# One 512-column matmul for two 256-column ones in the first block of a two-block transformer kernel

## The chip, the cores and the metric

The kernel runs on one core of one Trainium2 chip. The metric is device time in microseconds (us) of that core, from the first to the last instruction with what lies around them. Times are medians of several executions; the profile is of one further execution. PE is the matmul engine (TensorE), PEld its weight loads, DVE is VectorE, ACT is ScalarE, POOL is GpSimd, SP issues most transfers.

## What is computed

256 tokens of 2048 features go through two blocks. Only the first is touched by the change:

```python
z = rmsnorm(h, g) @ w_in                       # 2048 x 8704: conv, q, k, v and gate columns
y_a = (b_a * centred_dwconv3(c_a * v_a, w)) @ w_out_a      # 1024 x 2048
y_b = banded_window_attention(rope(q), rope(k), v, sink) @ w_o_attn   # 1024 x 2048
h = h + (sigmoid(gl_a + b) * y_a + sigmoid(gl_b + b) * y_b) @ w_mix_out
up = centred_dwconv3(rmsnorm(h, g2) @ ffn_w_up, w) + b     # 2048 x 11264
h = h + (silu(up[:, :5632]) * up[:, 5632:]) @ ffn_w_down   # 5632 x 2048
```

The second block has a convolution, attention and a layer of 16384 experts, of which each token takes 128.

## The kernel before

Everything is fp32. For the matmul each operand is cut into a high part (type fp32r, a copy by ScalarE) and a low part (the rest, a subtraction by VectorE), and a product is the sum of three: high by high, high by low and low by high. An activation chunk of 128 features lies in SBUF as 512 columns: 256 tokens of high parts, then 256 tokens of low parts. `split` (L263) and `prep` (L343) write it so.

Weights come as tiles of 512 KB (`wtile`, L400): 512 input by 256 output features. `wsplit` (L388) starts the transfer from SP (four buffers), copies the high part on ACT (L396) and subtracts on DVE (L397), into three buffers each. `gemm` (L411) takes one weight tile: for both halves `j` of 128 output features and four chunks `k` of 128 input features it calls `three` (L403), which issues three matmuls of 256 columns into the same 256 columns of PSUM, each with a weight load of its own: high weights by high activations (L405), high weights by low activations (L408), low weights by high activations (L409). These 24 matmuls use up one weight tile. `proj` (L420) makes 256 output features: four weight tiles (two for w_oa and w_ob), one PSUM bank of 512 columns (two halves of 256 tokens).

PSUM holds the pool `pmm` with four tiles of one bank, `psc` (two banks, attention scores) and `ptp` (two banks). A result leaves PSUM by one instruction in most places: `scaled` (L379) multiplies 512 columns by a factor per token on DVE; `add_residual` (L620) adds 512 columns to the residual `hT` on DVE; q and k are copied by ACT in halves (L557); the convolution's inputs and the outputs of w_oa and w_ob (L584, L585, L615, L616) are read by DVE where they are used.

The order of the first block is: k, q and v projections with rotation (L531 to L566); eight convolution projections, each with one unit of attention behind it (L581); four projections w_b (L589); eight rounds of w_ga, w_gb, w_oa, w_ob (L603); eight w_mix projections that update `hT` and prepare the next input (L627); the feed-forward part in six groups of 8, 8, 8, 8, 8 and 4 up-projections (L687). A group's down-projection (`down`, L663: eight outputs, each of two weight tiles, and of one in the last group) is issued after the first up-projection of the next group. Behind each of the last group's eight outputs stands `finish` (L676), which prepares the second block's input and two sums of squares. A scheduler fixes each engine's order when the program is built; on the chip each engine then works its queue in order.

The second block and the experts use the same `gemm` and the same pool (`proj`, `proj32`, `out_half` at L802, and the loop over the first expert table at L1039). The loop over the second expert table (L1220) has matmuls of 512, 512 and 448 columns into six banks.

Of the kernel before, what the change touches and what calls it, by code (L numbers as in the profile page):

```python
# [77 lines left out]
def arrange(inp):  # L78
    """Layout alone: the arrays that the program reads, by name."""
# [90 lines left out]
def constants():  # L170
    """Numbers that depend on shapes alone."""
# [34 lines left out]
def body(ctx: ExitStack, tc: tile.TileContext, a, out):  # L206
# [5 lines left out]
    pmm = pp.enter_context(tc.tile_pool(name="pmm", bufs=4, space=PSUM))  # L212
# [44 lines left out]
    def after(inst, other, wait=True):  # L257
        """inst waits for other, or only follows it on the same engine"""
# [13 lines left out]
    def rstd_of(v, pool, preload=True, out=None, lean=False):  # L272
        """v ** -0.5 with one Newton step; v [128, n] in SBUF; lean: less of it on the vector engine"""
# [26 lines left out]
    class MeanSquare:  # L300
        """mean of squares over the features, on all partitions: [128, T] in PSUM"""
# [4 lines left out]
        def feed(self, src, i, n=4, g=None):  # L306
            """chunks i * n to i * n + n of src, times g"""
# [35 lines left out]
    def prep(u, c, g):  # L343
        """chunk c of hT * g, split"""
# [4 lines left out]
    class Chunks:  # L349
        """[128, 16, 512] in two tiles"""  # L350
# [16 lines left out]
    def by_token(t, name):  # L367
        """[128, T], alike on all partitions -> [128 tokens, 2]"""
# [33 lines left out]

    def three(o, wh, wl, xh, xl, start, stop, behind=None):  # L403
        """o += w.T @ x without the product of the low parts"""
# [6 lines left out]
    def gemm(w, x, c0, ps, n_f, first, last, behind=None):  # L411
        """ps[:, j, :] += w[:, k, j].T @ x for 4 chunks of x from c0"""
# [7 lines left out]
    def proj(name, i, x, kt=4, c0=0):  # L420
        """256 features of a product, feature-major: [128, 2 * T] in PSUM"""
        ps = pmm.tile([P, 512], F32, tag="mm", name="ps_" + name)
# [4 lines left out]
    def proj32(name, i, x, g):  # L427
        """256 features of a product of x * g, x and the weights whole"""
        ps = pmm.tile([P, 512], F32, tag="mm", name="ps_" + name)
# [13 lines left out]
    def gemm_tok(w, x, c0, ps, col, f0, n, first, last):  # L443
        """ps[:, col + tt * n:][:n] += x[tt].T @ w[:, k, f0:f0 + n]: token-major"""
# [14 lines left out]
    def rope(src, dst, rotm, cos, sin):  # L459
        """dst = src * cos + rot(src) * sin, src in SBUF"""  # L460
# [65 lines left out]
    u = actin("u1")  # L526
    pk = pmm.tile([P, 512], F32, tag="mm", name="ps_k")
    for k in range(4):
        for c in range(4 * k, 4 * k + 4) if k < PREK else range(4 * k, DC) if k == PREK else ():
            prep(u, c, g_mix)  # L530
        gemm(wtile("w_kqv", k), u, 4 * k, pk, 2, k == 0, k == 3)  # L531
# [21 lines left out]
    for i in range(5):  # L553
        ps = proj("w_kqv", i, u) if i else pk
# [7 lines left out]
    ps = pmm.tile([P, 512], F32, tag="mm", name="ps_v")  # L562
    for k in range(4):
        gemm_tok(wtile("w_kqv", 20 + k), u, 4 * k, ps, 0, 0, 256, k == 0, k == 3)
    for tt in range(2):
        S.activation(vtok[:, tt], ps[:, tt * 256:(tt + 1) * 256], AF.Copy, scale=r1t[:, tt:tt + 1])  # L566

# [13 lines left out]
    for i in range(8):  # L581
        ps = proj("w_cv", i, u)
# [6 lines left out]
    for i in range(4):  # L589
        ps = scaled(proj("w_b", i, u), r1, "b_a")  # L590
# [12 lines left out]
    for i in range(8):  # L603
        pga = scaled(proj("w_ga", i, u), r1, "ga")
        pgb = scaled(proj("w_gb", i, u), r1, "gb")
        pya = proj("w_oa", i, ab, kt=2)
        pyb = proj("w_ob", i, ab, kt=2, c0=8)
        for j in range(2):
            c = 2 * i + j
            s = slice(j * T, (j + 1) * T)  # L610
            ga = tmp("g_a", "ta")
            S.activation(ga, pga[:, s], AF.Sigmoid, bias=bgate[:, c:c + 1])
            gb = tmp("g_b", "tb")
            S.activation(gb, pgb[:, s], AF.Sigmoid, bias=bgate[:, 16 + c:17 + c])
            V.tensor_tensor(ga, ga, pya[:, s], OP.mult)  # L615
            V.tensor_tensor(gb, gb, pyb[:, s], OP.mult)  # L616
            V.tensor_tensor(ga, ga, gb, OP.add)
            split(mix, c, ga)
# [44 lines left out]
    def down(gi, f, n, then=None):  # L663
        for i in range(8):
            ps = pmm.tile([P, 512], F32, tag="mm", name="ps_dn")
# [10 lines left out]
    def finish(i):  # L676
        """the input of the second block, of hT * g_fin"""
# [590 lines left out]
```

## Time and profile before

| | |
|---|---|
| runs (us) | 3041.73, 3041.75, 3043.57; median 3041.75 |
| span of the profiled execution | 3041.1 us |
| matmuls, weight loads | 22192, 22192 |
| PE, DVE, ACT, POOL busy | 98%, 76%, 50%, 28% of the span |
| mean granted TensorE clock | 0.996 |
| read from and written to HBM | 677.41 MB, 5.64 MB |

Busy time counts an engine from an instruction's start to its end. Matmuls are pipelined, so the duration of one (about 280 ns at 256 columns) is longer than the time from its start to the start of the next. What a stream of matmuls costs is read from the starts. A line of a helper stands for all of its calls, so groups are told apart by the tile that they write. Where a row says `x4`, it merges four instructions that follow each other.

### The profile page before, as it was taken

The numbers are of one execution on the slowest core, as the hardware profiler recorded it, in microseconds if no ns is written. First come the engines' busy times: TensorE is split into PE (matmuls) and PEld (weight loads), VectorE is DVE, ScalarE is ACT, GpSimd is POOL, SyncE is SP. The second block draws the span as 40 slices with busy tenths as digits, with TensorE's granted clock in tenths as the row PEclk, the third lists the DMA queues.
The fourth block names the chain that finished last, engine by engine and source line by source line (L and its number), as shares of the span: only waits on it lengthen the run. The fifth ranks groups of instructions, "written<-read, shape, count | busy, mean of one in ns | idle before, by whom it ended". The sixth has DMA issues, their size and how long they took to land.

```text
span 3041.1 us, 57181 instructions
## 1 busy us (share of the span) xinstructions
PE 2984.2 (98%) x22192; PEld 2825.3 (93%) x22192; DVE 2310.3 (76%) x4243; ACT 1529.6 (50%) x2229; POOL 866.0 (28%) x670
## 2 busy tenths in 40 slices
PE   8999999999999999999999999999999999999999
PEld 8889999999999999999988989999999897888887
DVE  6456555666666665668998788999997888999998
ACT  5454444554444444546555644555555554444444
POOL 0000000000000000000000055555554796777786
PEclk9999999999999999999999999999999999999999
DMA  6435555555555555554433678999999338999999
GB/s 220 147 121 182 184 181 186 182 180 182 185 183 183 185 181 185 182 182 165 154 110 126 212 248 298 318 321 325 324 319 330 124 135 299 337 332 339 330 335 319
DMA packets 211169, 686.81 MB, mean 226 GB/s; under 512 B 29264, under 2 KB 47056, under 8 KB 210512
## 3 DMA queue, kind: packets, MB, share of 16 engines
q1 hardware_dynamic: 169776, 523.15, 50.4%
q0 software_dynamic: 41120, 160.01, 15.3%
q8 instruction: 173, 2.83, 0.4%
q14 instruction: 100, 0.82, 0.1%
HBM read 677.41 MB, written 5.64 MB: 225 GB/s over the span
## 4 chain that ended last, share of the span: by engine, by line
PE 82%; DVE 6%; DMA 5%; issue 3%; POOL 2%; ACT 1%; POOLq 0%; SPq 0%; DVEq 0%; ACTq 0%
PE ps_w_up L408 6%; PE ps_w_up L409 6%; PE ps_w_up L405 6%; PE y L1240 5%; PE y L1239 5%; PE y L1238 5%; PE ps_u L409 3%; PE ps_u L405 3%; PE ps_dn L409 3%; PE ps_dn L405 3%; PE ps_dn L408 3%; PE ps_u L408 3%; DMA urows<-in_u_rows,ex 2%; PE ps_a L1160 2%; PE ps_sel L1121 1%
## 5 line engine op out<-in xcount | busy, mean ns | idle before, releaser
L397 DVE TENSOR_TENSOR wl<-wr,wh 128x1024 fp32r<-128x1024 f32 x572 | 700.6, 1225 | 403.0 <-ACT wh L396 397.5
L396 ACT ACTIVATE wh<-wr 128x1024 fp32r<-128x1024 f32 x572 | 606.3, 1060 | 739.3 <-PE ps_w_up L408 171.4
L907 POOL TENSOR_TENSOR tk_c<-tk_v 128x256 f32<-128x256 f32 x16 | 11.8, 740 | 1751.1 <-DVE tk_v L899 1750.9
L956 POOL DMA_INDIRECT vrows<-in_v_rows,ex x256 | 394.3, 1540 | 120.4 <-DVE yg L1207 59.6
L409 PE MATMUL ps_u<-u_a,ul 128*128 128x256 f32 x1408 | 401.5, 285 | 14.4 <-DVE ul L397 13.3
L408 PE MATMUL ps_u<-u_a,uh 128*128 128x256 f32 x1408 | 397.3, 282 | 0.4 <-issue 0.4
L405 PE MATMUL ps_u<-u_a,uh 128*128 128x256 f32 x1408 | 397.4, 282 | 0.1
L396 ACT ACTIVATE uh<-ur 128x512 fp32r<-128x512 f32 (+1 forms) x384 | 227.0, 598 | 237.9 <-DMA ur<-in_u_dense 91.7
L956 POOL DMA_INDIRECT urows<-in_u_rows,ex x228 | 268.3, 1177 | 214.7 <-PE ps_u L409 127.7
L1223 ACT ACTIVATE vhi<-vraw 128x1472 fp32r<-128x1472 f32 x128 | 184.1, 1438 | 263.8 <-PE y L1240 250.6
L1238 PE MATMUL y<-vhi,ah 128*128 128x512 f32 (+1 forms) x768 | 295.2, 384 | 3.5 <-ACT ah L1230 3.5
L1240 PE MATMUL y<-vhi,al 128*128 128x512 f32 (+1 forms) x768 | 298.4, 389 | 0.1
L1239 PE MATMUL y<-vlo,ah 128*128 128x512 f32 (+1 forms) x768 | 297.5, 387 | 1.0 <-DVE vlo L1226 1.0
L409 PEld LDWEIGHTS ps_u<-u_a,ul 128*128 128x128 f32 x1408 | 265.9, 189 | 21.9 <-DVE ul L397 20.2
L408 PE MATMUL ps_w_up<-u_a,wh 128*128 128x256 f32 x968 | 274.0, 283 | 0.0
L409 PE MATMUL ps_w_up<-u_a,wl 128*128 128x256 f32 x968 | 273.5, 282 | 0.0
L405 PE MATMUL ps_w_up<-u_a,wh 128*128 128x256 f32 x968 | 271.2, 280 | 0.0
L408 PEld LDWEIGHTS ps_u<-u_a,uh 128*128 128x128 f32 x1408 | 265.9, 189 | 0.9 <-issue 0.9
L405 PEld LDWEIGHTS ps_u<-u_a,uh 128*128 128x128 f32 x1408 | 265.9, 189 | 0.0
L397 DVE TENSOR_TENSOR ul<-ur,uh 128x512 fp32r<-128x512 f32 (+1 forms) x384 | 245.4, 662 | 20.4 <-ACT uh L396 17.5
L1226 DVE TENSOR_TENSOR vlo<-vraw,vhi 128x1472 fp32r<-128x1472 f32 x128 | 216.1, 1688 | 40.3 <-ACT vhi L1223 39.9
L1207 DVE SCALAR_TENSOR_TENSOR yg<-vrows,av,yg 128x576 f32<-128x576 f32 x256 | 208.5, 815 | 7.0 <-DMA vrows<-in_v_rows,ex 2.5
(413 smaller groups left out, 8623.6 us busy)
## 6 DMA issues: line engine op xcount, KB each, us to landing
vraw<-in_v_dense SPq DMA_DIRECT2D x128, 736.0 KB
wr<-in_w_up SPq DMA_DIRECT2D x176, 512.0 KB
ur<-in_u_dense SPq DMA_DIRECT2D x256, 256.0 KB
wr<-in_w_dn SPq DMA_DIRECT2D x88, 512.0 KB
ur<-in_u_dense SPq DMA_DIRECT2D x128, 192.0 KB
wr<-in_w_in SPq DMA_DIRECT2D x44, 512.0 KB
wr<-in_w_cv SPq DMA_DIRECT2D x32, 512.0 KB
wr<-in_w_ga SPq DMA_DIRECT2D x32, 512.0 KB
```

The costliest lines, as they stand in the source:

```text
L396: S.activation(hi, raw, AF.Copy)
L397: low.append(V.tensor_tensor(lo, raw, hi.bitcast(F32), OP.subtract))
L405: m = PE.matmul(o, wh, xh, start=start, stop=False, skip_group_check=True)
L408: PE.matmul(o, wh, xl, start=False, stop=False, skip_group_check=True)
L409: return PE.matmul(o, wl, xh, start=False, stop=stop, skip_group_check=True)
L956: g = G.indirect_dma_start(out=v, out_offset=None, in_=a[name], in_offset=bass.IndirectOffsetOnAxis(ap=ex[:, tt, s:s + 1], axis=0))
L1207: g = V.scalar_tensor_tensor(yg[:, tt], v, av[:, tt, s:s + 1], yg[:, tt], OP.mult, OP.add)
L1223: hi_op = S.activation(hi, raw, AF.Copy)
L1226: vlo.append(V.tensor_tensor(lo, raw, hi.bitcast(F32), OP.subtract))
L1238: PE.matmul(o, st, hi[:, c:c + n], start=e2 == 0, stop=False, skip_group_check=True)
L1239: PE.matmul(o, st, lo[:, c:c + n], start=False, stop=False, skip_group_check=True)
L1240: mm = PE.matmul(o, sl, hi[:, c:c + n], start=False, stop=e2 == P - 1, skip_group_check=True)
```

## The change

In the first block alone, the first two matmuls of `three` become one: high weights meet the high and the low activations in one matmul of 512 columns, which fills a whole PSUM bank. The third (low weights by high activations, 256 columns) is added into the second half of that bank. Two halves of output features take two banks, so an output of 256 features takes a tile of two banks and the pool `pmm` has two such tiles in place of four single ones. The halves of a bank are summed on the way out: `total` copies the second half of both banks to SBUF on ACT and adds the first half on DVE, 512 columns each; `scaled2` multiplies after that, in SBUF. `add_both` adds the two halves to the residual by two DVE instructions. The k projection, q, the convolution's inputs, w_b, w_ga, w_gb, w_oa, w_ob, w_mix, up and down go that way; v keeps three matmuls. In the gate loop the sigmoids now stand right behind each gate's projection. The second block and the experts keep `gemm` with three matmuls; their PSUM banks are now halves of a two-bank tile (`banks.get`), which comes free only when both halves have been read.

```diff
-    pmm = pp.enter_context(tc.tile_pool(name="pmm", bufs=4, space=PSUM))
+    pmm = pp.enter_context(tc.tile_pool(name="pmm", bufs=2, space=PSUM))
...
+    def scaled2(ps, rr, name):
+        t = total(ps, name)
+        t3 = t.rearrange("p (a b) -> p a b", a=2)
+        V.tensor_tensor(t3, t3, twice(rr), OP.mult)
         return t
...
+    class Halves:
+        def __init__(self):
+            self.t, self.k = None, 1
+        def get(self, name):
+            if self.k:
+                self.t = pmm.tile([P, 2, 512], F32, tag="mm", name=name)
+            self.k = 1 - self.k
+            return self.t[:, self.k]
...
+    def total(ps, name):
+        t = tm.tile([P, 512], F32, tag="td", name=name, bufs=3)
+        t3 = t.rearrange("p (a b) -> p a b", a=2)
+        S.activation(t3, ps[:, :, T:], AF.Copy)
+        V.tensor_tensor(t3, ps[:, :, :T], t3, OP.add)
+        return t
+
+    def gemm2(w, x, c0, ps, first, last):
+        hi, lo = w
+        for j in range(2):
+            for k in range(KC):
+                s = slice(k * FW + j * P, k * FW + (j + 1) * P)
+                PE.matmul(ps[:, j], hi[:, s], x[:, c0 + k, 0:2 * T], start=first and k == 0, stop=False,
+                          skip_group_check=True)
+                PE.matmul(ps[:, j, T:], lo[:, s], x[:, c0 + k, 0:T], start=False, stop=last and k == KC - 1,
+                          skip_group_check=True)
...
-            src = tmp("qk_s", "ta")
-            S.activation(src, ps[:, j * T:(j + 1) * T], AF.Copy)
+            src = t[:, j * T:(j + 1) * T]
...
-        ps = proj("w_cv", i, u)
+        ps = total(proj2("w_cv", i, u), "cv")
...
-        pya = proj("w_oa", i, ab, kt=2)
-        pyb = proj("w_ob", i, ab, kt=2, c0=8)
...
+        t = total(proj2("w_oa", i, ab, kt=2), "ya")
...
+    def add_both(ps, i):
+        d = hT[:, 2 * i:2 * i + 2]
+        V.tensor_tensor(d, d, ps[:, :, :T], OP.add)
+        V.tensor_tensor(d, d, ps[:, :, T:], OP.add)
...
-        add_residual(proj("w_mix", i, mix), i)
+        add_both(proj2("w_mix", i, mix), i)
...
-                gemm(wtile("w_dn", gi * 16 + i * kt + k), f, KC * k, ps, 2, k == 0, k == kt - 1)
-            add_residual(ps, i)
+                gemm2(wtile("w_dn", gi * 16 + i * kt + k), f, KC * k, ps, k == 0, k == kt - 1)
+            add_both(ps, i)
...
-            ps = scaled(proj("w_up", up0 + i, u), r2, "up")
+            ps = scaled2(proj2("w_up", up0 + i, u), r2, "up")
```

## Rows read from the trace of the kernel before

**Rows 1.** The page: the length of the span, part 1 (busy time of the matmul engine), and two lines of part 2 (busy tenths, and granted TensorE clock in tenths, in 40 slices of 76 us each).

```profile
span 3041.1 us, 57181 instructions
...
PE 2984.2 (98%) x22192; PEld 2825.3 (93%) x22192; DVE 2310.3 (76%) x4243; ACT 1529.6 (50%) x2229; POOL 866.0 (28%) x670
...
PE   8999999999999999999999999999999999999999
...
PEclk9999999999999999999999999999999999999999
```

**Rows 2.** The page, part 4, the chain that ended last: shares of the span by engine, then by line.

```profile
PE 82%; DVE 6%; DMA 5%; issue 3%; POOL 2%; ACT 1%; POOLq 0%; SPq 0%; DVEq 0%; ACTq 0%
PE ps_w_up L408 6%; PE ps_w_up L409 6%; PE ps_w_up L405 6%; PE y L1240 5%; PE y L1239 5%; PE y L1238 5%; PE ps_u L409 3%; PE ps_u L405 3%; PE ps_dn L409 3%; PE ps_dn L405 3%; PE ps_dn L408 3%; PE ps_u L408 3%; DMA urows<-in_u_rows,ex 2%; PE
```

**Rows 3.** Windows: busy us of each engine in a stretch with the number of instructions (x), then granted clock, DMA share and GB/s. The gate and output stage with its neighbours (235 to 546), w_mix (546 to 640), the feed-forward part (640 to 1380), its last down-projection (1380 to 1403), two stretches of the second block, then one stretch of the dense expert products with the first table and one with the second.

```profile
235.00:546.00 311.00, 311.00 (x2594) 311.00 (x2594) 176.74 (x222) 136.67 (x162) 0.00 (x0) 1.00 0.55 183
546.00:640.00 94.00, 94.00 (x785) 94.00 (x785) 58.73 (x76) 48.27 (x59) 0.00 (x0) 1.00 0.56 183
640.00:1380.00 740.00, 739.36 (x6152) 738.59 (x6150) 475.91 (x609) 344.07 (x434) 0.00 (x0) 1.00 0.55 183
1380.00:1403.00 23.00, 20.71 (x167) 20.26 (x168) 20.08 (x33) 18.95 (x36) 0.00 (x0) 1.00 0.38 131
1403.00:1560.00 157.00, 156.85 (x1197) 145.72 (x1195) 144.92 (x273) 97.11 (x169) 0.00 (x0) 1.00 0.45 148
1560.00:1730.00 170.00, 162.53 (x1137) 146.84 (x1136) 141.36 (x284) 98.33 (x188) 0.00 (x0) 0.97 0.43 145
...
2100.00:2300.00 200.00, 195.23 (x1619) 192.81 (x1618) 180.92 (x445) 109.11 (x179) 114.99 (x97) 1.00 0.95 325
...
2700.00:2900.00 200.00, 200.00 (x897) 166.26 (x896) 183.33 (x176) 98.09 (x75) 151.21 (x100) 1.00 0.94 335
```

**Rows 4.** Windows of one source line each (PE only), from the start to the last matmul of the first block: line 405, then line 408, then line 409. Columns: busy us (x instructions), granted clock, DMA share, GB/s.

```profile
0.00:1402.72 1402.72, 1037.71 (x3680) 1.00 0.54 179
...
0.00:1402.72 1402.72, 1041.97 (x3680) 1.00 0.54 179
...
0.00:1402.72 1402.72, 1041.78 (x3680) 1.00 0.54 179
```

**Rows 5.** Timeline of PE in the up-projection: start in us, duration, engine, line, operation. Between the first and the last row lie 18 starts-to-starts without one left out.

```profile
799.81 0.28 PE L405 MATMUL ps_w_up<-u_a,wh 128*128 128x256 f32 x1
799.93 0.28 PE L408 MATMUL ps_w_up<-u_a,wh 128*128 128x256 f32 x1
800.05 0.28 PE L409 MATMUL ps_w_up<-u_a,wl 128*128 128x256 f32 x1
...
801.97 0.28 PE L405 MATMUL ps_w_up<-u_a,wh 128*128 128x256 f32 x1
```

**Rows 6.** Timeline of PE in the second expert product: the first of three 448-column matmuls, of the three 512-column ones after them, of the next three 512-column ones, and of the next three 448-column ones.

```profile
2750.36 0.36 PE L1238 MATMUL y<-vhi,ah 128*128 128x448 f32 x1
...
2750.97 0.39 PE L1238 MATMUL y<-vhi,ah 128*128 128x512 f32 x1
...
2751.67 0.39 PE L1238 MATMUL y<-vhi,ah 128*128 128x512 f32 x1
...
2752.36 0.36 PE L1238 MATMUL y<-vhi,ah 128*128 128x448 f32 x1
```

**Rows 7.** Timeline of PE in the first expert product, 256 columns: 24 starts-to-starts lie between the two rows.

```profile
2260.06 0.28 PE L405 MATMUL ps_u<-u_a,uh 128*128 128x256 f32 x1
...
2262.91 0.28 PE L405 MATMUL ps_u<-u_a,uh 128*128 128x256 f32 x1
```

**Rows 8.** Timeline of PE at the very start, 256 columns: 17 starts-to-starts lie between the two rows.

```profile
9.95 0.41 PE L409 MATMUL ps_k<-u_a,wl 128*128 128x256 f32 x1
...
13.57 0.41 PE L408 MATMUL ps_k<-u_a,wh 128*128 128x256 f32 x1
```

**Rows 9.** Groups by line, engine and form: a ScalarE copy of 512 columns out of PSUM, then three VectorE operations on 512 columns (the scaling of an up-projection's output, an addition in SBUF alone, the residual addition out of PSUM). Columns: busy us, mean ns of one, idle before it and what ended that.

```profile
L511 ACT ACTIVATE at_pt<-ps_pt 128x512 f32<-128x512 f32 x28 | 15.4, 586 | 5.4 <-PE ps_pt L509 5.4
...
L622 DVE TENSOR_TENSOR hT<-hT,ps_dn 128x512 f32<-128x512 f32 x48 | 32.9, 686 | 27.6 <-PE ps_dn L409 27.4
L382 DVE TENSOR_TENSOR up<-ps_w_up,r 128x512 f32<-128x512 f32 x44 | 30.4, 692 | 30.0 <-PE ps_w_up L409 30.0
...
L318 DVE TENSOR_TENSOR sq_sq<-sq_sq,sq 128x512 f32<-128x512 f32 x6 | 4.1, 684 | 0.7 <-ACT sq L312 0.7
```

**Rows 10.** Waits: who waited for whom, us in total, times, longest. First a row of the whole span, then the list of PE's own waits from 1376 to 1404 us (two of its three rows).

```profile
ACT wh L396 <- PE ps_w_up L408: 171.4, 97, 1.9
...
PE ps_dn L405 <- ACT ff L265: 1.5, 1, 1.5
PE ps_dn L409 <- DVE wl L397: 1.2, 1, 1.2
```

**Rows 11.** Timeline of VectorE around the end of the first block: start, duration, line, operation, in brackets the idle time before it and what ended it.

```profile
1386.21 1.28 DVE L622 TENSOR_TENSOR hT<-hT,ps_dn 128x512 f32<-128x512 f32 x2
...
1405.89 0.87 DVE L346 SCALAR_TENSOR_TENSOR u_b<-hT,c_g,u_b 128x256 fp32r<-128x256 f32 x2
...
1412.62 1.23 DVE L397 TENSOR_TENSOR wl<-wr,wh 128x1024 fp32r<-128x1024 f32 x1 [1.05 <-ACT wh L396]
...
1424.57 0.69 DVE L382 TENSOR_TENSOR ag<-ps_w_in,r 128x512 f32<-128x512 f32 x1
```

More of the change, by code (lines that the diff above doesn't have):

```diff
@@ L401, in wtile, with fresh, wide, proj2 @@
         return wsplit(a[name][i], wp, KC * FW, "w", 4, 3)
+    class Halves:
[6 more added lines that the diff above has]
+            return self.t[:, self.k]
+        def fresh(self):
+            self.k = 1
+    banks = Halves()
+    def wide(name):
+        return pmm.tile([P, 2, 512], F32, tag="mm", name=name)
+    def total(ps, name):
[3 more added lines that the diff above has]
+        V.tensor_tensor(t3, ps[:, :, :T], t3, OP.add)
+        return t
+    def gemm2(w, x, c0, ps, first, last):
[7 more added lines that the diff above has]
+                          skip_group_check=True)
+    def proj2(name, i, x, kt=4, c0=0):
+        ps = wide("ps_" + name)
+        for k in range(kt):
+            gemm2(wtile(name, i * kt + k), x, c0 + KC * k, ps, k == 0, k == kt - 1)
+        return ps
     def three(o, wh, wl, xh, xl, start, stop, behind=None):
@@ L420, in proj @@
     def proj(name, i, x, kt=4, c0=0):
-        ps = pmm.tile([P, 512], F32, tag="mm", name="ps_" + name)
+        ps = banks.get("ps_" + name)
         for k in range(kt):
@@ L427, in proj32 @@
     def proj32(name, i, x, g):
-        ps = pmm.tile([P, 512], F32, tag="mm", name="ps_" + name)
+        ps = banks.get("ps_" + name)
         for kt in range(DC // KC):
@@ L526, in body @@
     u = actin("u1")
-    pk = pmm.tile([P, 512], F32, tag="mm", name="ps_k")
+    pk = wide("ps_k")
     for k in range(4):
@@ L553, in body @@
     for i in range(5):
[L554 removed]
+        t = total(proj2("w_kqv", i, u) if i else pk, "qk_s")
         for j in range(2):
[L556 to L557 removed]
+            src = t[:, j * T:(j + 1) * T]
             if i == 0:
@@ L561, in body @@
                 rope(src, qT[:, 2 * (i - 1) + j], rotm1, rope1[:, 2], rope1[:, 3])
-    ps = pmm.tile([P, 512], F32, tag="mm", name="ps_v")
+    ps = banks.get("ps_v")
     for k in range(4):
@@ L566, in body @@
         S.activation(vtok[:, tt], ps[:, tt * 256:(tt + 1) * 256], AF.Copy, scale=r1t[:, tt:tt + 1])
+    banks.fresh()
     V.memset(cvp[:, :, 0:1], 0.0)
@@ L589, in body @@
     for i in range(4):
-        ps = scaled(proj("w_b", i, u), r1, "b_a")
+        ps = scaled2(proj2("w_b", i, u), r1, "b_a")
         if i == 0:
@@ L603, in body @@
     for i in range(8):
-        pga = scaled(proj("w_ga", i, u), r1, "ga")
-        pgb = scaled(proj("w_gb", i, u), r1, "gb")
-        pya = proj("w_oa", i, ab, kt=2)
-        pyb = proj("w_ob", i, ab, kt=2, c0=8)
-        for j in range(2):
[L609 to L618, printed above, removed]
+        gs = []
+        for name, tag, o, act_in in (("ga", "ta", 0, "w_ga"), ("gb", "tb", 16, "w_gb")):
+            t = scaled2(proj2(act_in, i, u), r1, name)
+            for j in range(2):
+                g = tmp("g_" + name, tag)
+                S.activation(g, t[:, j * T:(j + 1) * T], AF.Sigmoid, bias=bgate[:, o + 2 * i + j:o + 2 * i + j + 1])
+                gs.append(g)
+        t = total(proj2("w_oa", i, ab, kt=2), "ya")
+        for j in range(2):
+            V.tensor_tensor(gs[j], gs[j], t[:, j * T:(j + 1) * T], OP.mult)
+        t = total(proj2("w_ob", i, ab, kt=2, c0=8), "yb")
+        for j in range(2):
+            V.tensor_tensor(gs[2 + j], gs[2 + j], t[:, j * T:(j + 1) * T], OP.mult)
+            V.tensor_tensor(gs[j], gs[j], gs[2 + j], OP.add)
+            split(mix, 2 * i + j, gs[j])
     def add_residual(ps, i):
@@ L664, in down @@
         for i in range(8):
-            ps = pmm.tile([P, 512], F32, tag="mm", name="ps_dn")
+            ps = wide("ps_dn")
             kt = n // KC
             for k in range(kt):
-                gemm(wtile("w_dn", gi * 16 + i * kt + k), f, KC * k, ps, 2, k == 0, k == kt - 1)
-            add_residual(ps, i)
+                gemm2(wtile("w_dn", gi * 16 + i * kt + k), f, KC * k, ps, k == 0, k == kt - 1)
+            add_both(ps, i)
             if then:
@@ L802, in out_half @@
     def out_half(i, h, behind=None):
-        ps = pmm.tile([P, 512], F32, tag="mm", name="ps_out2")
+        ps = banks.get("ps_out2")
         for k in range(2):
@@ L1039, in body @@
     for i in range(64):
-        ps = pmm.tile([P, 512], F32, tag="mm", name="ps_u")
+        ps = banks.get("ps_u")
         for b in range(2):
```

2 lines of the change are left out of this document (1 added, 1 removed).

## The prediction

> **What bounds the kernel now.** I read the page first: PE is busy for 98% of the span, in every slice after the first, and its clock is granted in full in all of them [rows 1]. The chain of waits says the same of the path: 82% of it is PE, and the up-projection's three lines have 6% each [rows 2]. Busy time alone doesn't say that PE is at its limit, so next come the windows of the stages. From 235 to 1380 us PE and its weight loads are both busy without a gap, while DVE is at 57 to 64%, ACT at 44 to 51% and the transfers at about 183 GB/s; with the first expert table the same transfers reach 325 GB/s [rows 3]. So in the first block nothing but the stream of matmuls sets the time, and a nanosecond saved per matmul is one saved at the end. Its length is known: each of the lines 405, 408 and 409 ran 3680 times until 1402.72 us [rows 4].
>
> The last view is the timeline, for the distance between starts, since durations overlap. In the up-projection 18 distances take 801.97 - 799.81 = 2.16 us: 120 ns for a 256-column matmul [rows 5]. 3 x 3680 x 0.120 = 1325 us of the first block's 1403 are these matmuls; the rest is the start, v, attention and the rotations.
>
> **The matmuls.** The change takes away 3680 matmuls of 256 columns with their weight loads and makes 3680 others 512 wide; the columns streamed stay the same. What goes is only what a matmul costs beyond its columns. I need the distance of a 512-column matmul in a stream. The first block has none, but the second expert product has: three of 448 columns take 2750.97 - 2750.36 = 0.61 us (203 ns each), and six of 512 take 2752.36 - 2750.97 = 1.39 us (232 ns each) [rows 6]. From 448 to 512 columns that is 0.44 ns a column; carried on down to 256 columns it gives 232 - 256 x 0.44 = 119 ns, against 120 measured. So the three sizes lie on one line, 0.44 ns a column and some 7 to 8 ns for each matmul. Those rows come from a stage with 335 GB/s of transfers [rows 3], which could have slowed them; but 256 columns take 2.85 / 24 = 119 ns at 325 GB/s [rows 7] and 120 at 183, so transfers don't set the distance. I take 231 ns for 512 columns, as the two threes give 233 and 230.
>
> So a triple of 3 x 120 = 360 ns becomes 231 + 120 = 351: 9 ns less, x 3680 = 33 us. The bounds: with 232 and 119 for 512 columns and the slope's 256, the fixed part is 6 ns and the gain 22 us. If the whole excess of the 256-column matmul over 256 / 2.4 = 107 ns is a fixed part, it is 13 ns and the gain 49 us. I stand on 9, as it comes from 512-column rows themselves. In the first microseconds the 17 distances of 3.62 us are 213 ns, as 256 columns take at 1.2 GHz (though the clock column prints full clock there) [rows 8]; those few triples gain nothing, under 0.1 us in all.
>
> **The way out of PSUM.** `total` is new at 93 outputs (5 of k and q, 8 convolution, 4 w_b, 32 of the gate rounds, 44 up): an ACT copy of 512 columns, 0.59 us by the nearest row out of PSUM, and one more DVE operation on 512 columns, 0.68 us whether it reads PSUM or SBUF [rows 9]. `add_both` makes 56 residual additions (48 down, 8 w_mix) into two, 0.6 us more each, as two in a row take 1.28 [rows 11]. In an up-projection of 32 x 351 ns = 11.2 us that puts DVE from 64% to about 71% and ACT from 46% to 53% [rows 3]. Nothing of it is on PE's path as long as two things hold. First, weight halves must be ready: ACT's copy of a tile waits for the matmuls three tiles back, 97 times and 1.8 us each time in the up-projection alone [rows 10], so ACT idles between tiles, and a split that starts then is due two tiles (5.6 us) later; 0.59 us of ACT and 0.69 of DVE ahead of it fit. Second, with two wide tiles in place of four single ones, PE needs an output's banks again one output later: 11.2 us where an output has four weight tiles, 5.6 where it has two; the new chain (copy 0.59, addition 0.69, behind at most a split of 1.2) is about 2.5. I cost both at zero; without that cover it would be up to 1.3 us for each of the 93 outputs (in the rivals). The rotations of q and k wait 0.7 us longer, twice in each of 5 outputs, but stand in PE's queue inside the next projection; zero to 4 us, taken at 0.5, as the scheduler can move them.
>
> **Where a wait grows.** The last down-projection has no cover. Its first output needs the last chunk of the up-projection just before; PE waits 1.5 us there today, for ACT's copy of the high part [rows 10]. The chain that it waits for gets the new copy (0.59) and one DVE operation (0.69) longer: 1.3 us more. Then come eight outputs of one weight tile each (2.8 us), with `finish` behind each. DVE is 20.1 of 23 us busy there [rows 3] and gets 8 x 0.6 = 4.8 us more. What is late then: the last prepared chunks, ready at 1406.7 [rows 11], are due for the fourth weight tile of the next projection, at 1402.7 + 3 x 2.88 = 1411.4, so PE has 4.7 us to give. DVE itself has small gaps after that, as 1.05 us at 1412.6 [rows 11], which take up part; but then the second block runs DVE at 92% until 1560 [rows 3], and what is not taken up moves its end. Between 0 and 4.8 us; I take 2.5, half. The two-deep PSUM can also make PE wait for `add_both` here, inside the same 4.8 us. Second block and experts: halves of a tile come free in pairs, so PE runs three outputs ahead in the worst case where it ran four; zero, with up to 3 us where DVE is the late one (1403 to 1730).
>
> **The sum.** -33 + 0.5 + 1.3 + 2.5 = -29 us. The profiled span is 3041.1 and the median of the runs 3041.75, 0.7 us more, so I take it off the median: 3013. The forecast's own range is 3005 (230 ns, a gain of 37, no costs) to 3033 (the gain of 22, costs at their upper ends of 4, 1.3, 4.8 and 3, 13 in all).
>
> **The rivals.**
> (a) *The price goes by columns.* If the excess at 256 columns (120 - 107 = 13 ns) doubles with the columns, 512 take 240 ns, nothing is saved, and the costs stay: 3046. For it: at the start 256 columns take 213 ns, exactly 256 / 1.2, with no fixed part at all [rows 8]. Against: 512 columns run at 232, not 240 [rows 6].
> (b) *A small fixed part.* Between that zero and the 6 ns above, nearer to zero, lie some 2 ns a triple: -7 + 4 gives 3039 us. The same rows speak for it and against it. The Trainium skill has a rule for this, in "TensorE: Matmul & The Clock Gate", section "Back-to-back issue gap": columns / 2.4 plus 2.5 ns at full clock. By that rule a triple would go from 328 to 325 ns, 9 us in all and 3037 at the end; the trace doesn't agree, with 120 ns where the rule has 109 [rows 5] and 232 where it has 216 [rows 6].
> (c) *Weight loads bound the stream.* If 120 ns is what a weight load takes and 512 columns hide it, the triple is 213 + 120 = 333 ns: -99 + 4 gives 2946. For it: PEld is without a gap too [rows 3], and the excess is gone where the columns are slow [rows 8]. Against: at 448 and 512 columns, where a load of 120 ns is well hidden, 17 and 18 ns of excess are still there [rows 6]. The section "LDWEIGHTS (loading the stationary operand)" of the same page of the Trainium skill gives 107 ns for 128 columns, which is the shape of this rival. A fixed 13 ns (2997) stands between it and my forecast.
> (d) *Slower: the new copy delays the weights.* ACT and DVE work their queues in order. If the scheduler puts `total`'s copy, which waits for an output's last matmul, ahead of the next weight tiles' copies, the splits come late. It decides at 33 / 93 = 0.36 us of PE wait for each output with a `total`: below, the change still gains. At 0.59 us, the copy's length, it is 55 us: 3042 + 55 - 29 = 3068. For it: DVE waits for ACT's high part in every tile, so both move together. Against: ACT's own waits of 1.8 us a tile [rows 10] and the two tiles of lead.
>
> **How the numbers follow.** Forecast 0.70; (a) 0.08; (b) 0.06; the fixed 13 ns 0.05 and (c) 0.04, so 0.09; (d) 0.07. A measurement of this kernel can tell about 0.2%, 6 us, from no change. Faster by more than that: the forecast and (c) with its neighbour, 0.79; within it: (a) and (b), 0.14; slower: (d), 0.07. The range takes in the forecast's own range, the fixed 13 ns and (b): 2996 to 3039; outside are (c), (a) and (d), 0.19.
>
> **What would show it.** After the change the timeline of the up-projection should have starts alternating by 231 and 120 ns, 32 pairs in 11.2 us; 18512 matmuls in all; 235 to 1380 us still without a gap on PE and about 28 us shorter; the transfers there near 188 GB/s. Pairs of 360 ns would be (a), 357 (b), 333 (c). Waits of PE for `wh` or `wl` inside that stretch would be (d), and waits for `total` or `add_both` would show two wide tiles to be too few. The wait at the last down-projection should be 2.8 us, and DVE's backlog there should show as a later first scaling of the second block, counted from the last matmul of the first. I am wrong if the pair is off by more than 4 ns, or if PE gets a regular wait.

## The result, and the profile after

| | runs | median (us) | lowest to highest |
|---|---|---|---|
| before | 4 | 3042.66 | 3041.73 to 3047.45 |
| after | 4 | 3070.14 | 3060.76 to 3072.48 |

The ratio is 1.0082, with a 95% interval from 1.0066 to 1.0099: the change makes the kernel slower, by 27 us between the medians. The forecast was 3013 us, and the range ended at 3039.

The page of the kernel after, first: the span, part 1, and the engines' shares of the chain. It answers to [rows 1] and [rows 2].

```profile
span 3070.7 us, 50080 instructions
...
PE 2956.3 (96%) x18512; PEld 2631.2 (86%) x18512; DVE 2407.2 (78%) x4392; ACT 1573.6 (51%) x2312; POOL 875.2 (29%) x670
...
PE 87%; DVE 4%; ACT 3%; DMA 3%; issue 1%; POOL 1%; DVEq 0%; SPq 0%; POOLq 0%; ACTq 0%
```

There are 18512 matmuls, 3680 fewer, as predicted. But PE is busy for 96% of a longer span where it had 98%, and ACT has 3% of the chain where it had 1%. Which stages do that? The windows, as in [rows 3]: gate and output stage, w_mix, up-projection, last down-projection, two stretches of the second block, first expert table.

```profile
235.00:546.00 311.00, 311.00 (x1783) 272.06 (x1782) 207.33 (x276) 160.41 (x207) 0.00 (x0) 1.00 0.60 189
546.00:640.00 94.00, 94.00 (x540) 82.61 (x540) 63.30 (x75) 48.86 (x59) 0.00 (x0) 1.00 0.60 188
640.00:1336.00 696.00, 696.00 (x3990) 608.99 (x3989) 508.33 (x669) 353.47 (x462) 0.00 (x0) 1.00 0.60 189
1336.00:1375.50 39.50, 28.05 (x132) 22.43 (x131) 32.04 (x53) 25.23 (x46) 0.00 (x0) 0.87 0.32 95
1375.50:1606.00 230.50, 221.64 (x1520) 195.12 (x1519) 206.12 (x428) 130.53 (x266) 0.00 (x0) 0.96 0.41 131
1606.00:1718.00 112.00, 106.58 (x851) 103.49 (x850) 82.95 (x126) 63.45 (x87) 0.00 (x0) 1.00 0.52 166
1829.00:2394.00 565.00, 510.70 (x4154) 503.04 (x4153) 466.65 (x1131) 282.34 (x461) 297.36 (x244) 0.98 0.88 295
```

Up to 1336 us everything is as forecast: no gap on PE, DVE at 73% and ACT at 51% in the up-projection, 189 GB/s. From there on PE has gaps: 11 us of 39.5 in the last down-projection and 54 us of 565 with the first expert table, whose transfers run at 295 GB/s where they had 320 over the same table (before, 1833 to 2364 us). The up-projection's timeline answers to [rows 5].

```profile
799.78 0.39 PE L444 MATMUL ps_w_up<-u_b,wh 128*128 128x512 f32 x1
800.01 0.28 PE L446 MATMUL ps_w_up<-u_b,wl 128*128 128x256 f32 x1
800.13 0.39 PE L444 MATMUL ps_w_up<-u_a,wh 128*128 128x512 f32 x1
```

A pair takes 350 ns. A table of milestones shows where the gain went; each is the start of the first or the last matmul of a stage in the two traces.

| | before | after | difference |
|---|---|---|---|
| last matmul of the up-projection starts | 1375.7 | 1336.1 | -39.6 |
| last matmul of the last down-projection | 1402.7 | 1375.5 | -27.2 |
| first matmul of the first expert table | 1833.3 | 1820.1 | -13.2 |
| last matmul of that table | 2364.2 | 2395.1 | +30.9 |
| last matmul of the second table | 3035.9 | 3065.4 | +29.5 |

The first expert table's beginning needs care, as halves are handed out in turn: its first output lies in the second half of a tile that a projection of the keys began, and goes by that tile's name, `ps_w_pq`. The rows are the table's first group of matmuls before the change, then after it the first output's and the last group of the others.

```profile
L405 PE MATMUL ps_u<-u_a,uh x1408: 274/281/415, 1833.3 to 2363.9; 128*128 128x256 f32 x176
...
L457 PE MATMUL ps_w_pq<-u_a,uh x22: 274/281/366, 1820.1 to 1828.4; 128*128 128x256 f32 x22
...
L461 PE MATMUL ps_u<-u_a,ul x1386: 274/281/416, 1829.0 to 2395.1; 128*128 128x256 f32 x198
```

So the stream gives 39.6 us, and three stages take 70.5: the last down-projection 12.4, the second block with the experts' keys 14.0, the first expert table 44.1. The lists of PE's waits in these three stages (1320 to 1420 us, then 1375.5 to 1828.8, then 1828 to 2394) show waits that the kernel before doesn't have, or has shorter:

```profile
PE ps_dn L444 <- DVE ff L266: 3.4, 1, 3.4
PE ps_dn L444 <- DVE hT L679: 2.8, 5, 1.3
PE ps_w_in L457 <- ACT sq L312: 2.1, 1, 2.1
PE ps_dn L444 <- DVE up L435: 1.8, 1, 1.8
PE ps_dn L446 <- DVE wl L403: 1.3, 1, 1.3
...
PE ps_sub L1058 <- ACT kq L1054: 5.9, 5, 1.5
PE ps_out L457 <- DVE hT L674: 3.8, 6, 1.7
PE ps_w_in L457 <- DVE kv_s L382: 1.2, 1, 1.2
...
PE ps_u L457 <- ACT ha L1111: 54.2, 31, 4.4
```

The last row is the largest: 31 waits, in a loop of 64 outputs, of which 62 share 31 two-bank tiles. The kernel before has no such wait; its largest in that loop is `PE ps_u L409 <- DVE ul L397: 13.3, 21, 1.3`. The timeline after the change shows what PE waits for (PE's last matmul of one output, a weight split and the copy of that output on ACT, PE's first matmul of the next output).

```profile
2007.46 0.28 PE L461 MATMUL ps_u<-u_a,ul 128*128 128x256 f32 x1
...
2007.66 0.63 ACT L402 ACTIVATE uh<-ur 128x512 fp32r<-128x512 f32 x1 [0.54 <-PE ps_u L460]
...
2008.20 1.05 ACT L1111 ACTIVATE ha<-ps_u 128x512 f32<-128x512 f32 x1
2009.31 0.38 PE L457 MATMUL ps_u<-u_a,uh 128*128 128x256 f32 x1 [1.57 <-ACT ha L1111]
```

PE has finished the first half of a tile and does not begin the second half before ACT has read the first. Between tiles there is no such wait, hence one for every second output. In front of the copy ACT has a weight split, which waited for PE itself.

### The profile page after: what moved, and what is told of

Read it like the earlier page. It is cut to its first block, busy times and chain, and to the rows that moved or that the text cites. A ratio compares the mean times of both kernels' runs of the same rounds, so it can differ in the third digit from the quotient of the medians.

```text
span 3070.7 us, 50080 instructions
## 1 busy us (share of the span) xinstructions
PE 2956.3 (96%) x18512; PEld 2631.2 (86%) x18512; DVE 2407.2 (78%) x4392; ACT 1573.6 (51%) x2312; POOL 875.2 (29%) x670
## 4 chain that ended last, share of the span: by engine, by line
PE 87%; DVE 4%; ACT 3%; DMA 3%; issue 1%; POOL 1%; DVEq 0%; SPq 0%; POOLq 0%; ACTq 0%
PE ps_w_up L444 11%; PE y L1297 5%; PE ps_w_up L446 5%; PE y L1296 5%; PE y L1295 5%; PE ps_dn L444 5%; PE ps_u L457 5%; PE ps_u L460 5%; PE ps_u L461 4%; PE ps_dn L446 3%; PE ps_w_cv L444 2%; PE ps_w_ga L444 2%; PE ps_w_gb L444 2%; PE ps_w_mix L444 2%; PE ps_a L1217 2%
## 5 line engine op out<-in xcount | busy, mean ns | idle before, releaser
L461 PE MATMUL ps_u<-u_a,ul 128*128 128x256 f32 x1386 | 394.3, 285 | 0.1
L1013 POOL DMA_INDIRECT urows<-in_u_rows,ex x228 | 279.6, 1226 | 257.9 <-PE ps_u L461 200.2
L444 PE MATMUL ps_w_up<-u_a,wh 128*128 128x512 f32 x968 | 342.8, 393 | 0.0
L403 DVE TENSOR_TENSOR ul<-ur,uh 128x512 fp32r<-128x512 f32 (+1 forms) x384 | 253.1, 672 | 72.0 <-ACT uh L402 71.1
L444 PE MATMUL ps_dn<-ff,wh 128*128 128x512 f32 x704 | 248.3, 396 | 8.0 <-DVE ff L266 3.4
L1283 DVE TENSOR_TENSOR vlo<-vraw,vhi 128x1472 fp32r<-128x1472 f32 x128 | 216.1, 1688 | 39.6 <-ACT vhi L1280 39.5
L444 PEld LDWEIGHTS ps_w_up<-u_a,wh 128*128 128x128 f32 x968 | 181.4, 187 | 43.5
```

Of the source, the lines that this page charges most:

```text
L403: low.append(V.tensor_tensor(lo, raw, hi.bitcast(F32), OP.subtract))
L444: PE.matmul(ps[:, j], hi[:, s], x[:, c0 + k, 0:2 * T], start=first and k == 0, stop=False, skip_group_check=True)
L461: return PE.matmul(o, wl, xh, start=False, stop=stop, skip_group_check=True)
L1013: g = G.indirect_dma_start(out=v, out_offset=None, in_=a[name], in_offset=bass.IndirectOffsetOnAxis(ap=ex[:, tt, s:s + 1], axis=0))
L1283: vlo.append(V.tensor_tensor(lo, raw, hi.bitcast(F32), OP.subtract))
```

## Theory and rivals after the result

Theory: merging the matmuls brings what was forecast. It is lost (1) because outputs that share a tile of two banks are treated as one buffer, so the second output's first matmul waits for the first one's reader, in the second block and the first expert table, which still use three matmuls; and (2) in the last down-projection, where nothing covers the new additions, the longer chain to `ff` and PSUM that is two deep.

Rivals: the extra ACT and DVE work itself delays later stages; the merged matmuls or the clock cost something later; within (2), one cause alone is the whole.

## Experiments

Times of the runs are beside the kernel before on the same chip: 3044.49 us (3041.74 to 3048.37, 7 runs) for the first four, 3042.89 (3037.55 to 3050.08, 9 runs) for the last four.

**1. Single banks again behind the first block.** The merged matmuls and all of the first block stay; only the later stages get four single banks back.

```diff
-    pmm = pp.enter_context(tc.tile_pool(name="pmm", bufs=2, space=PSUM))
+    pw = ExitStack()
+    pmm = pw.enter_context(tc.tile_pool(name="pmm", bufs=2, space=PSUM, reuse_waits="tile"))
...
         def get(self, name):
+            if singles:
+                return pmm.tile([P, 512], F32, tag="mm", name=name)
...
     down(len(GROUPS) - 1, f, GROUPS[-1], finish)
+    pw.close()
+    pmm = pp.enter_context(tc.tile_pool(name="pm1", bufs=4, space=PSUM, reuse_waits="tile"))
+    singles.append(1)
```

> The changed kernel, but when the first block ends the pool of two-bank tiles is closed and a pool of four single-bank tiles takes its place for the second block and the experts. Theory (pairing): a matmul into the second half of a two-bank tile waits until the first half has been read, which costs about 35 us in the first expert table (31 waits of PE for the copy of ps_u) and most of the 25 us that the second block gives back; so about 3010 us, between 3000 and 3025, with no wait of ps_u for that copy, and the first expert table back to 531 us from its first to its last matmul. Rival (lateness): the second block is late because VectorE comes out of the last down-projection with a backlog and PE with a lower clock, and the expert loop because its queue order changed; then the banks matter little and the time stays above 3050.

Measured: 3023.29 us (3018.01 to 3027.39), ratio 0.9935 [0.9919, 0.9952]. The milestones' differences are -38.8 (up-projection), -26.0 (last down), -22.9 and -23.6 (first table, first and last matmul), -25.0 at the end. PE's waits with the first table (1805 to 2345 us):

```profile
PE ps_u L465 <- DVE ul L404: 13.0, 19, 3.4
PE ps_sl L1097 <- ACT ef L1098: 1.1, 1, 1.1
```

The wait for `ha` is gone, and what is left is the wait of the kernel before. Two of the three losses are nearly gone with it: 14.0 + 44.1 us became 3.1 - 0.7, and the table takes 530.2 us from its first to its last matmul. (The 35 us of the expectation were counted from the table's second output.) The option `reuse_waits` came in with the new pools; experiment 4 does without it. The first block's extra ACT and DVE work is unchanged here, so it is not what delays the later stages.

**2. Pairs of banks in the kernel before.** The opposite: three 256-column matmuls everywhere, no new work on ACT or DVE, but each output takes half of a two-bank tile.

```diff
-    pmm = pp.enter_context(tc.tile_pool(name="pmm", bufs=4, space=PSUM))
+    pmm = pp.enter_context(tc.tile_pool(name="pmm", bufs=2, space=PSUM))
...
-        ps = pmm.tile([P, 512], F32, tag="mm", name="ps_" + name)
+        ps = banks.get("ps_" + name)
```

> The kernel before, with three 256-column matmuls everywhere, but its four single banks replaced by two tiles of two banks whose halves are handed out in turn. Nothing of the first block's arithmetic is changed. Theory (pairing): the waits between the halves come with the banks alone; the first expert table gets 30 to 40 us longer, the second block 5 to 25, and the first block loses up to 1 us per pair of outputs where a reader is late; 3077 to 3110 in all. Rival (lateness): without the longer way out of PSUM nothing is late, and the time is that of the kernel before, 3036 to 3048.

Measured: 3160.56 us (3154.80 to 3166.14), ratio 1.0377 [1.0357, 1.0398]. PE's waits over the span:

```profile
PE ps_u L417 <- ACT ha L1066: 51.0, 30, 3.8
PE ps_dn L417 <- DVE hT L634: 19.5, 22, 1.6
PE ps_w_up L417 <- DVE up L394: 19.2, 22, 0.9
...
PE ps_w_ga L417 <- DVE ga L394: 7.0, 8, 0.9
PE ps_sub L1013 <- ACT kq L1009: 5.9, 5, 1.5
```

The pairing alone makes the same wait for `ha`, and up to the end of the first block it costs 64 us (63.7 by its last matmul): 44 waits in the 92 outputs of the up- and down-projections and 8 in 16 gate projections, close to one for every second output. From there to the end of the first table it takes 56.8 us more (13.1 up to the table, 43.7 with it), as it did after the change (14.0 and 44.1). The time lies above the forecast of the experiment, as the first block pays more than was thought. The cause is shown from both sides.

**3. The merge undone alone.** The kernel after with its evacuation, its additions and its tiles, but two matmuls of 256 columns in place of the one of 512.

```diff
-                PE.matmul(ps[:, j], hi[:, s], x[:, c0 + k, 0:2 * T], start=first and k == 0, stop=False,
+                PE.matmul(ps[:, j, :T], hi[:, s], x[:, c0 + k, 0:T], start=first and k == 0, stop=False,
+                          skip_group_check=True)
+                PE.matmul(ps[:, j, T:], hi[:, s], x[:, c0 + k, T:], start=False, stop=False,
```

> The changed kernel, with the 512-column matmul cut in two of 256 columns again (high weights by high activations into the first half of the bank, by low activations into the second); banks, sums and everything else as changed. If the merged matmul saves 10 ns a pair (360 against 350 ns, 3680 times), the first block gets 36 us longer and the whole about 3106 (3098 to 3112). If the price goes by columns, nothing changes: 3065 to 3075.

Measured: 3111.50 us (3109.07 to 3115.08), ratio 1.0218 [1.0201, 1.0235]. The last matmul of the up-projection starts 0.6 us earlier than before the change. So all the new work of ACT and DVE costs the stream nothing, and the merge alone is worth 39 us by then and 41 at the end (3111.5 - 3070.1). The last down-projection takes 39.1 us here, so what slows it is not the merged matmul either. PE's waits there (1370 to 1416 us) are close to those of the kernel after, but the first is for ACT's copy of the high part:

```profile
PE ps_dn L444 <- ACT ff L265: 2.6, 1, 2.6
PE ps_dn L444 <- DVE hT L681: 2.4, 4, 1.2
PE ps_w_in L459 <- ACT sq L312: 2.1, 1, 2.1
PE ps_dn L444 <- DVE up L435: 1.8, 1, 1.8
```

**4. Two single-bank tiles in place of one of two banks.** The same banks and columns, but each bank is a buffer of its own; `total` and `add_both` then work on each half of the features by itself.

```diff
-        return pmm.tile([P, 2, 512], F32, tag="mm", name=name)
+        return [pmm.tile([P, 512], F32, tag="mm", name=name) for _ in range(2)]
```

> The changed kernel with four single-bank tiles throughout: an output of 256 features takes two single tiles, and the way out is done for each half of features by itself (two ScalarE copies and two VectorE additions of 256 columns in place of one each of 512; four residual additions in place of two). Theory (pairing): no waits between halves are left anywhere, so the 36 us of the matmul stream are kept but for the last down-projection, where VectorE gets 1 us more for each of 8 outputs; 3010 to 3025. Rival (lateness): VectorE has more to do than in the changed kernel, so the second block starts later still: 3070 or more.

Measured: 3021.16 us (3018.45 to 3022.32), ratio 0.9922 [0.9905, 0.9938]; the differences are -40.0, -25.9, -23.1, -22.5 and -21.5. The waits for `ha` are gone here too, though the banks are the same ones. The wait belongs to the tile as the unit of the program's synchronization; nothing in these runs shows that the banks themselves need it. The last down-projection stays as slow (41.1 us).

Four more runs take apart that stretch, from the last matmul of the last up-projection to the last of the last down-projection: 27.0 us before, 39.4 after, 39.8 in experiment 1, on which three of them build. The timeline of the kernel after shows its beginning (rows of DVE and PE).

```profile
1338.55 0.68 DVE L435 TENSOR_TENSOR up<-ps_w_up,up 128x512 f32<-128x512 f32 x1
...
1339.29 0.50 PE L444 MATMUL ps_dn<-ff,wh 128*128 128x512 f32 x1 [1.84 <-DVE up L435]
...
1343.56 0.43 DVE L266 TENSOR_TENSOR ff<-ff_s,ff 128x256 fp32r<-128x256 f32 x1 [0.48 <-ACT ff L265]
1344.04 0.80 PE L444 MATMUL ps_dn<-ff,wh 128*128 128x512 f32 x1 [3.42 <-DVE ff L266]
...
1344.85 0.63 PE L444 MATMUL ps_dn<-ff,wh 128*128 128x512 f32 x1
1345.27 0.41 PE L446 MATMUL ps_dn<-ff,wl 128*128 128x256 f32 x1
1345.49 0.63 PE L444 MATMUL ps_dn<-ff,wh 128*128 128x512 f32 x1
```

PE waits first for the addition out of the last up-projection's PSUM, then for the low part of the last chunk. The merged matmul needs high and low activations at once, so it waits for DVE's subtraction, 0.43 us behind ACT's copy, where the kernel before waited for that copy alone [rows 10]. After the longer wait pairs stand 640 ns apart.

**5. The last up-projection alone on the old way.** Three matmuls into the first bank, one scaling from PSUM, which shortens the chain to `ff`.

```diff
-            ps = scaled2(proj2("w_up", up0 + i, u), r2, "up")
+            if up0 + i == 43:
+                pl = wide("ps_last")[:, 0]
+                for k in range(4):
+                    gemm(wtile("w_up", 4 * 43 + k), u, 4 * k, pl, 2, k == 0, k == 3)
+                ps = scaled(pl, r2, "up")
+            else:
+                ps = scaled2(proj2("w_up", up0 + i, u), r2, "up")
```

> The version with single banks after the first block, and in it the last up-projection (number 43 of 44) alone back on the old way: three 256-column matmuls into the first bank of its tile, one scaling straight from PSUM. Takes away only the longer chain to the last ff chunk. Theory (the last down-projection's 12 us are a sum of three things: the chain to ff, DVE's second additions, the two tiles of PSUM): PE's wait for ff falls from 3.4 us to about 1.5 to 2, the other waits stay, 1 to 3 us less than the version it is made from, some 3021. Rival (the wait for ff is the start of it all: the clock falls because of it, and the late matmuls make the rest): the granted clock stays full through the last down-projection, and 8 to 12 us go, some 3013.

Measured: 3019.62 us (3017.93 to 3026.76), ratio 0.9922 [0.9907, 0.9937]. The wait for `up` is gone, but the one for `ff` is 3.2 us where 3.4 were and 1.5 to 2 were expected (PE arrives at it earlier). The stretch takes 38.7 us: one microsecond of twelve. About the rival this run says little, as the wait that it blames is still there, and the granted clock of the stretch is 0.83. Experiment 6 settles it.

**6. One addition in the last down-projection, PSUM still two deep.** Three matmuls into the first bank of each tile, one residual addition.

```diff
-                gemm2(wtile("w_dn", gi * 16 + i * kt + k), f, KC * k, ps, k == 0, k == kt - 1)
-            add_both(ps, i)
+                wt = wtile("w_dn", gi * 16 + i * kt + k)
+                if then:
+                    gemm(wt, f, KC * k, ps[:, 0], 2, k == 0, k == kt - 1)
...
+                add_residual(ps[:, 0], i)
```

> The version with single banks after the first block, and in it the last down-projection's eight outputs back on three 256-column matmuls into the first bank of a two-bank tile, with one residual addition each in place of two; still two tiles of PSUM. Takes away DVE's eight extra additions (0.6 us each, 4.8 us) and leaves the depth. Theory of the sum: the waits for hT get shorter, 3 to 6 us less, some 3019. Rival (DVE's additions are all of it): 10 to 12 us less, some 3012. Rival (the depth of two tiles is all of it): less than 2 us, some 3022.

Measured: 3020.08 us (3016.83 to 3022.43), ratio 0.9925 [0.9909, 0.9941]. The stretch falls to 30.6 us, 9.2 less, and the waits for `hT` (2.8 us in experiment 1) and for `wl` (3.9) are gone. The wait for `ff` is still 3.0 us, so it is not the start of it all. But only 3 us show in the time, and those lie inside the intervals of the two ratios. In the trace the lead of 35.8 us at the end of the first block shrinks to 28.0 at the first expert table; 2.8 us of that are waits for DVE's `wl`. In 50 us of the second block (from 1563 us) the granted clock is 0.86, where experiment 7 has 0.93 (from 1558 us); how much of the rest that is was not settled.

**7. The last down-projection wholly as before.** Experiment 1 with the change of pools moved ahead of it: four single banks, three matmuls, one addition.

```diff
+    pw.close()
+    pmm = pp.enter_context(tc.tile_pool(name="pm1", bufs=4, space=PSUM, reuse_waits="tile"))
+    singles.append(1)
+    down(len(GROUPS) - 1, f, GROUPS[-1], finish)
...
-            add_both(ps, i)
+            (add_residual if singles else add_both)(ps, i)
```

> The version with single banks, the change of the PSUM pool moved ahead of the last down-projection: its eight outputs have four single banks, three 256-column matmuls and one residual addition, as in the kernel before. Only the longer chain to the last ff chunk stays. Theory of the sum: 8 to 11 us less, some 3013, with the wait for ff of some 3 us left. If the wait for ff and the clock after it are the cause, it stays at 3020 or more.

Measured: 3010.32 us (3007.68 to 3010.63), ratio 0.9889 [0.9872, 0.9907]: 13 us less than experiment 1, and the intervals of the two ratios lie apart. The stretch takes 29.3 us, 2.3 more than before the change. The wait for `ff` is 0.7 us where some 3 were expected; PE comes to it later, behind matmuls at the lower clock (last section).

**8. Experiment 4 with the last up- and the last down-projection on the old way.** Everything behind the last up-projection is then as before the change.

```diff
-            ps = wide("ps_dn")
+            ps = banks.get("ps_dn") if then else wide("ps_dn")
...
-            add_both(ps, i)
+            (add_residual if then else add_both)(ps, i)
...
-            ps = scaled2(proj2("w_up", up0 + i, u), r2, "up")
+            ps = scaled(proj("w_up", up0 + i, u), r2, "up") if up0 + i == 43 else scaled2(proj2("w_up", up0 + i, u), r2, "up")
```

> The version whose wide outputs are two single-bank tiles with an evacuation for each half, and in it the last up-projection and the last down-projection on the old way (three matmuls, one bank, one scaling or addition). Everything after the last up-projection but one is as in the kernel before. Theory: the stream's gain of about 38 us stays to the end: 3042.5 - 38 = 3004 to 3008. If something else than pairing of banks and the last down-projection takes the gain back, it stays near 3020.

Measured: 3008.88 us (3002.08 to 3010.79), ratio 0.9889 [0.9871, 0.9907], just above the 3004 to 3008 that were expected. The windows of the stretch, each from the last matmul of the up-projection to the last of the first block: experiment 1, experiment 6, experiment 7, this one.

```profile
1336.90:1376.70 39.80, 27.79 (x130) 22.42 (x129) 32.93 (x53) 26.11 (x48) 0.00 (x0) 0.87 0.33 96
```
```profile
1336.30:1366.90 30.60, 25.79 (x194) 25.06 (x194) 23.30 (x40) 21.85 (x40) 0.00 (x0) 0.89 0.39 121
```
```profile
1336.30:1365.60 29.30, 25.35 (x193) 24.36 (x192) 24.16 (x39) 21.85 (x40) 0.00 (x0) 0.94 0.42 127
```
```profile
1336.00:1363.10 27.10, 24.19 (x195) 23.42 (x194) 23.41 (x39) 21.26 (x39) 0.00 (x0) 1.00 0.45 138
```

Read downwards they are the sum: 9.2 us for the second additions (with the merged matmuls, which by experiment 3 are not what costs), 1.3 for PSUM two deep in place of four, 2.2 for the last up-projection's chain, and 27.1 us is the stretch of the kernel before. The last step also goes from the base of experiment 1 to that of experiment 4. This last kernel and experiment 7 are the fastest of the study, 33 to 34 us below the kernel before; in this one's profiled execution the lead of 39.7 us stays to the end (-40.6), though that execution was the fastest of its four.

## Why the prediction was wrong

**The matmul term was right, and a little small.** From the first matmul of the up-projection to its last, with the five down-projections between, stand 2048 triples in 739.2 us before (361 ns) and 2048 pairs in 716.7 after (350 ns). The pair was forecast at 351; the triple was taken at 360. 11 ns for the 3616 triples up to there are 39.7 us, and -39.6 were measured. Rivals (a), (b) and (c) fell with this pair; theirs were 360, 357 and 333. The Trainium skill's formula in "TensorE: Matmul & The Clock Gate", section "Back-to-back issue gap", which the section gives for a matmul by itself, comes to some 2.5 ns a triple, an estimate from it; the rows have 11.

**"I cost both at zero" was right for the evacuation inside the first block.** From 235 to 1336 us the list of PE's waits is empty, and experiment 3 adds all the new work of ACT and DVE for 0.6 us less than before at the end of the up-projection. Rival (d) forecast 3068, close to the 3070 measured, by a mechanism that did not occur: no wait for `wh` or `wl` in that stretch. The time alone would have spoken for it.

**The step that failed: "halves of a tile come free in pairs, so PE runs three outputs ahead in the worst case where it ran four; zero, with up to 3 us".** I counted buffers and took the halves as independent until they are freed. They are not: the second half can't be begun while the first is being read. So PE runs no output ahead inside a tile and waits for the reader at every second output. It cost 58 us in place of 0 to 3: 14.0 in the second block and the keys, 44.1 in the first expert table, a stage to which the 3 us, for a late DVE up to 1730 us, gave nothing. There PE's waits grow by some 40 us (54.8 against 14.6 from the table's first matmul to its last). Experiments 1, 2 and 4 show it, and the prediction's own sign, a regular wait of PE, came. The diff's own words, "which comes free only when both halves have been read", had put me on the release of a tile; the question that I left out was what its second half waits for. The price could then have been bounded: between two outputs of a tile PE idles for the reader's time at least, and the copy of `ha` took 1.10 us in the kernel before, which for 31 tiles is 34 us:

```profile
L1054 ACT ACTIVATE ha<-ps_u 128x512 f32<-128x512 f32 x64 | 70.2, 1096 | 4.6 <-PE ps_u L409 4.6
```

The 31 waits came to 1.75 us each, with a split in front of the copy in the timeline above, and the waits for `ul` of the kernel before (13.3 us) went.

The Trainium skill says in "Perfetto Trace Analysis", section "Matmuls", that independent groups of matmuls should rotate through different PSUM banks, so that the evacuation of one lies beside the matmuls of the next. After the change they still rotate through different banks, and the evacuation no longer overlaps inside a tile: here the rule needs separate buffers as well as separate banks.

**The last down-projection was sized at 1.3 + 2.5 and cost 12.4 us.** The place was named, and so were its three causes. The chain to `ff` was sized at 1.3 and is 2.2 in experiment 7 against 8, 1.1 in experiment 5; the wait for `ff` was forecast at 2.8 us and is 3.4. The additions and the depth were put together at 0 to 4.8 and are 9.2 and 1.3. The bound of 8 x 0.6 counted DVE's time alone. With DVE late, PE waits for `hT` and `wl` in turn, and after its longest wait the clock is lower for a while; the bound left both out. Nor does DVE's backlog show as a later first scaling of the second block: it begins 15.3 us after the first block's last matmul (1390.83 us), where 21.9 had been [rows 11]; PE had waited for DVE inside the stretch. How much of this stretch reaches the end isn't settled: of experiment 6's 9.2 us some 3 arrived, of experiment 7's 10.5 all (13).

**The rest.** The rotations of q and k cost next to nothing: the convolution's projections begin 1.8 us earlier, and 160 triples of 11 ns are 1.8. Behind the first table the two kernels run alike (1.4 us). The sum: -39.6 + 12.4 + 14.0 + 44.1 - 1.4 = 29.5 us, the difference of the two profiled executions' last matmuls. The kernel that 3013 described, with nothing lost to the pairing, is that of experiments 1 and 4, at 3023 and 3021; only with the last stretch on the old way as well does it run at 3009 to 3010.

## What to carry to other kernels

When a change turns several buffers into parts of one, don't only count how many are left: ask for each part what its first writer waits for, because in these programs the tile is the unit of waiting, and a reader of one part holds up the writer of another. Look beyond the stage that the change is made for, at every stage that draws from the same pool, and first at those where PE already waits now and then. And where a stream of matmuls is long, gapless and full of pairs with the same weights, the merge is worth the 11 ns a time that it brought here; end it one step before the stream ends, where nothing covers the evacuation.

## What the runs showed of the hardware

The granted clock falls within the last down-projection, where PE waits 3.4 us. Two windows of the kernel after:

```profile
1340.00:1345.00 5.00, 1.58 (x7) 1.16 (x6) 2.69 (x6) 1.92 (x4) 0.00 (x0) 0.56 0.24 92
1345.00:1350.00 5.00, 5.00 (x24) 4.22 (x23) 2.33 (x3) 1.98 (x4) 0.00 (x0) 0.75 0.00 0
```

PE is busy for 1.58 of 5 us and the granted clock there is 0.56; behind the wait pairs stand 640 ns apart, which is 768 columns at 1.2 GHz, and from 1347.8 us on some 350 again. The five pairs from 1344.04 to 1347.41 take 3.4 us where 1.75 are due, so the wait of 3.4 us and the slow pairs behind it cost some 5.0.

Which wait brings the clock down there isn't settled, as one of 1.8 us ends 1.3 us before the other begins. In experiment 5 the 3.2 us for `ff` come alone, and pairs stand some 640 ns apart behind them. In experiment 7 the clock falls behind the 1.8 us, while PE is at work: from 1340.34 us on 256-column matmuls stand 213 ns apart, as at 1.2 GHz, and the clock of the stretch is 0.94.

```profile
1340.34 0.41 PE L461 MATMUL ps_dn<-ff,wh 128*128 128x256 f32 x1
1340.56 0.41 PE L464 MATMUL ps_dn<-ff,wh 128*128 128x256 f32 x1
1340.77 0.41 PE L465 MATMUL ps_dn<-ff,wl 128*128 128x256 f32 x1
```

With the 1.5 and 1.2 us of the kernel before [rows 10] it is full [rows 3].

A 512-column and a 256-column matmul with a weight load each take 230 and 120 ns also at 183 to 189 GB/s of transfers; the straight line of [rows 6] held in another stage.
